# Rotary tables from eight transposes, their rows copied to the partitions by DMA, and one ordering dependence on VectorE

## The chip, the cores and the metric

The kernel runs on one core of one Trainium2 chip. The metric is the device time of one execution in microseconds (us). The engines of a core are TensorE (PE: matmuls and transposes; PEld: its weight loads), VectorE (DVE), ScalarE (ACT), GpSimd (POOL) and SyncE (SP, which here issues all DMAs). PSUM, where PE writes, has eight banks; several parts of the kernel compete for them.

## The reference

One decoder block on x of 1024 tokens by 1024 channels, float32:

```python
h = rms_norm(x, g_attn_pre) * (1 + sc_a) + sh_a      # sc_a, sh_a, ...: silu(c) @ w_ada + b_ada
proj = h @ w_in                                      # 1024 -> 2304
qa, ka = partial_rope(...), partial_rope(...)        # mixer A: 8 query heads, 2 key heads
qb, kb = partial_rope(...), partial_rope(...)        # mixer B: 8 heads
...                                                  # windowed attention A (sinks), dilated mixture B
x = x + gt_a * rms_norm(concat(norm(oa), norm(ob)) @ w_out, g_attn_post)
h = rms_norm(x, g_mlp_pre) * (1 + sc_m) + sh_m
x = x + gt_m * rms_norm(square(relu(h @ w_up)) @ w_down, g_mlp_post)
```

What the change touches is the rotation. It turns 16 of the 64 channels of each query and key head, by cos and sin of position times eight frequencies:

```python
rot = concat([x1 * cos - x2 * sin, x2 * cos + x1 * sin])   # x1, x2: 8 channels each
```

## The kernel before

**Precision.** Each float32 operand of a matmul is split into a high part (rounded on ScalarE) and a low part (the rest, by VectorE or GpSimd). A product is three matmuls: high by high, low by high, high by low (L875, L876, L878 in the projections).

**Layout.** Projections put channels on partitions and tokens on the free axis. The columns of w_in are ordered so that the channels to be rotated, of queries and keys alike, lie in the first of the three 128-channel chunks (c = 0) of each of six units u (two of mixer A, four of mixer B). Tokens go in two halves x = 0, 1 of 512. The rotation (f_rope, L768 to L775) is four VectorE instructions with two tables `tabs[0]` (cos) and `tabs[1]` (plus and minus sin), each 128 partitions by 1024 tokens, with the scale of the scores (-0.125 for queries, 1 for keys) multiplied in. Partitions that aren't rotated have cos 1 and sin 0, times that scale.

**The tables.** cos and sin are computed with tokens on partitions: `cosw` (128 x 8 blocks x 8 frequencies) and `sinw`, which holds minus sin at index 0 and sin at 1. `tables()` (L712 to L735) turns them. For each i (0: cos, 1: sin) GpSimd fills a tile "rows" of 128 x 8 x 128 by a memset and 8 to 10 copies of 64 elements (L719, L725), one for each place to which a frequency goes; PE transposes each of the eight blocks, four to a PSUM bank "ptab" (L731), and ScalarE copies a bank into the table with the scale of its partition (L733). This is done twice: before the first unit, for mixer A's order of channels (units 0 and 1), in the two PSUM banks of tag "t"; and before unit 2, for mixer B's order, in the bank of tag "x". The first transposes wait for `e_hh[3, 1]`, the high part of the fourth channel chunk. Each call makes four groups of four transposes and four ScalarE copies.

**The planner.** The order of each engine's instructions is fixed when the program is built, by a small planner (`Sched`). Each step has a duration, events it waits for (deps), buffers that it takes and gives back (`Res`, such as r_t for the two "t" banks), and a prio. For ACT, DVE, POOL and SP it picks the step with the earliest start, then the lowest prio, then the oldest. PE has named streams, each first in, first out; among streams whose head is ready, the order is post, misc, mod, fin, xt, tab, then dense ahead of or behind the attention. A step that can't have its buffer isn't ready. While PE would idle before the first matmul of the second token half, dummy matmuls on ones ("fillers", L892) are put in.

**The start, to about 70 us.** The x blocks come in, ScalarE squares them, GpSimd computes rstd (L467, L469), and PE transposes the scaled blocks into banks "t" (L640, stream xt), which ScalarE or VectorE copies to xnT (L644). The modulation is computed in four groups of two channel chunks: VectorE sums w_ada times silu(c) (L660, L662: four steps of two instructions), PE reduces over partitions (L670), VectorE finishes scale and shift (L676 to L678), then ScalarE writes the high part hw (L699, event e_hh) and the full value (L696), both with prio 0, and VectorE the low part (L702, event e_hl). The first group of chunks (k = 0, 1) is done for each token half by itself, the others for both. The first unit (first_unit) accumulates six results at once, x = 0, 1 by c = 0, 1, 2, in six PSUM banks; its order is x = 0 with k = 0, 1, then x = 1 with k = 0, 1, then k = 2 to 5 for all, then k = 6, 7 accumulator by accumulator. The sixth accumulator (x = 1, c = 2) is one of the two "t" banks:

```python
acc_at = [(pj, "pj", r_pj)] * 2 + [(po, "o", r_o)] + [(psp, "s", r_s)] * 2 + [(pt, "t", r_t)]
```

**After that** projections of the next units run beside the attention of earlier ones (to about 360 us), then the output projection, then the MLP as a fast matrix product with seven multiplications. SP issues all loads and stores in the planner's order: weights (w_st, L540), modulation weights (wa, L520; wa_st, L1008), parts of queries and keys sent to their places (kt, qt, L818).

Of the kernel before, what the change touches and what calls it, by code (L numbers as in the profile page):

```python
# [19 lines left out]
P = 128  # L20
# [304 lines left out]
def t_ps(n):  # L325
    return 0.055 + 0.00083 * n
# [10 lines left out]
def t_dv(n):  # L337
    return 0.066 + 0.00104 * n
# [19 lines left out]
def hybrid_block(ctx: ExitStack, tc: tile.TileContext, x, positions, w_ada, b_ada, g_attn_post, w_in, w_out,  # L358
# [128 lines left out]
    def r_in(a):  # L487
        return r_stg if a in beside else r_wa
# [125 lines left out]
    e = op("DVE", 4.2, f_turns, [e_pos, e_c], prio=1)  # L614

    def f_sin():
        A.activation(sinw[:, :, 1], ang[:], AF.Sin)
        A.activation(cosw[:], kq[:], AF.Sin)
    e_xn, e_rs = [[], []], []
    e_sin = op("ACT", 0.5, f_sin, [e, e_sinset], prio=1)  # L620
    e_rope = op("DVE", 0.15, lambda: V.tensor_scalar(sinw[:, :, 0], sinw[:, :, 1], -1.0, None, ALU.mult), [e_sin],
                prio=1)

    def x_block(tb):
# [21 lines left out]
                                    gives=[(r_t, 1)], prio=2))  # L646

    e_hh, e_hl = {}, {}
    def mod_group(g):

        b = {}
        e = e_cond
        c = slice(2 * g, 2 * g + 2)
        for j in range(4):
            def f(j=j):
                for n in range(2):
                    w, cj = wa_t[g, j][:, 512 * n:512 * n + 512], cond[:, 2 * j + n:2 * j + n + 1]
                    if j == n == 0:
                        b["acc"] = p0.tile([P, 512], F32, name="acc_a", tag="acc_a", bufs=2)
                        V.tensor_scalar(b["acc"][:], w, cj, None, ALU.mult)  # L660
                    else:
                        V.scalar_tensor_tensor(b["acc"][:], w, cj, b["acc"][:], ALU.mult, ALU.add)  # L662
# [24 lines left out]
    def mod_chunk(k, eg, half):  # L687
        t0, t1 = (0, TB) if half is None else (4 * half, 4 * half + 4)
        n = (t1 - t0) * P
        h = xnT[:, k, t0 * P:t1 * P].rearrange("p (x t) -> p x t", t=512)  # L690
        hh, hl = (hw[:, t0 // 4 * 4 + k // 2:t1 - 3 + k // 2:4, i, k % 2 * 512:k % 2 * 512 + 512] for i in range(2))
        deps = [eg] + (e_xn[0] + e_xn[1] if half is None else e_xn[half])

        def full(eng):
            if eng is A:
                return lambda: A.activation(h, h, AF.Identity, bias=s_a[:, k:k + 1], scale=g_a[:, k:k + 1])  # L696
            return lambda: V.tensor_scalar(h, h, g_a[:, k:k + 1], s_a[:, k:k + 1], ALU.mult, ALU.add)

        eh = op("ACT", t_sb(n) + 2 * AP_COST, lambda: A.activation(hh, h, AF.Identity, bias=s_a[:, k:k + 1],  # L699
                                                                  scale=g_a[:, k:k + 1]), deps, prio=0)  # L700
        e = op("ACT", t_sb(n) + 2 * AP_COST, full(A), [eh], prio=0)
        e = op("DVE", t_dv(n), lambda: V.tensor_tensor(hl, h, hh.bitcast(F32), ALU.subtract), [e],  # L702
               prio=0)
        for x in (0, 1) if half is None else (half,):
            e_hh[k, x], e_hl[k, x] = eh, e

# [2 lines left out]
    for g in range(4):  # L709
        mod_group(g)  # L710

    def tables(groups, place, r_place, r_bank, bank, deps):  # L712

        for i in range(2):
            b = {}

            def f_rows(i=i, b=b):
                t = b["t"] = place(i)
                G.memset(t, 0.0 if i else 1.0)  # L719
                for o, step, h in groups:  # L720
                    for x in range(2):
                        src = sinw[:, :, 1 - x] if i else cosw[:]
                        o_ = o + 64 * x
                        for j in range(h):
                            G.tensor_copy(t[:, :, o_ + j * step:o_ + j * step + (8 * h - h) * step + 1:h * step], src)  # L725
            e = op("POOL", 4.0, f_rows, [e_rope] + e_rs, takes=[(r_place, 1)] if r_place else [], prio=0)
            for x in range(2):
                def f_t(x=x, b=b):
                    b[x] = bank()
                    for j in range(4):  # L730
                        T.transpose(b[x][:, j], b["t"][:, 4 * x + j], ident)  # L731
                d = pe_op("tab", 0.43, f_t, [e, e_hh[3, 1]], takes=[(r_bank, 1)], gives=[(r_place, 1)] if x and r_place else [])
                e_tab[x].append(op("ACT", t_ps(512) + AP_COST, lambda i=i, x=x, b=b: A.mul(  # L733
                    tabs[i][:, 512 * x:512 * x + 512], b[x][:].rearrange("p b t -> p (b t)"), scl[0]), [d] + deps[x],
                                   gives=[(r_bank, 1)], prio=2))  # L735

    e_tab = [[], []]
    tables([(0, 2, 4), (1, 8, 1)], lambda i: vring.tile([P, TB, P], F32, name="rows", tag="v"), r_v, r_t,
           lambda: pt.tile([P, 4, P], F32, name="ptab", tag="t"), [[], []])


    op("ACT", 1.6, lambda: A.activation(warm[:], nhalf[:], AF.Exp), [e_sin] + [e_hl[KC - 1, x] for x in range(2)],
# [224 lines left out]

# [1211 lines left out]
```

## Time and profile before

| | |
|---|---|
| median of 3 runs (lowest to highest) | 1128.47 us (1128.34 to 1129.39) |
| the profiled execution: time | 1129.15 us |
| the profiled execution: span of its instructions | 1127.1 us |
| mean granted TensorE clock | 0.996 |
| table transposes (L731) | 32, 272 ns median |
| table copies on ScalarE (L733) | 8, 688 ns median |
| "rows" on GpSimd: memsets, copies | 4 and 36 |
| DMA | 193.69 MB, all issued by SP |

How to read it: a line of a timeline gives start, length, engine, line of the kernel, operation, output <- inputs, shape and count, and in brackets how long the engine idled before it and which instruction ended that. A matmul's length (390 ns for 512 columns) is longer than the distance to the next, because matmuls overlap; the distance from start to start is what one costs. A line of a tile view gives lowest, median and highest duration in ns. The table of stretches gives the busy time of PE, the granted clock, the share of DMA and GB/s.

### The profile page before, as it was taken

Reading aid. Unit: us, or ns where it says so; the run is one execution under the profiler, and the core shown is the slowest. Engines: PE = TensorE matmul, PEld = TensorE weight load, DVE = VectorE, ACT = ScalarE, POOL = GpSimd, SP = SyncE. Lnnn points to the kernel's source line nnn. Section 1 sums busy time; section 2 is a strip of 40 time slices with the busy share of each in tenths; the row PEclk is TensorE's granted clock in tenths of the full one; section 3 lists DMA queues with packets and bytes.
Section 4 is the critical chain, followed back from the end, with each engine's and each line's share of the span. In section 5 each row is a group of like instructions: output and inputs, shape, how many; then the busy total and the mean of one; then the engine's idle time right before and its main releaser. Section 6 shows DMA issues by size and latency. Waiting matters only on the chain.

```text
span 1127.1 us, 15613 instructions
## 1 busy us (share of the span) xinstructions
PE 1107.0 (98%) x5417; PEld 920.9 (82%) x5417; DVE 817.2 (73%) x1379; ACT 636.8 (56%) x1111; POOL 255.4 (23%) x336
## 2 busy tenths in 40 slices
PE   8999999999999999999999999999999999999997
PEld 6788888888888788788888888888888888888885
DVE  7968767666686576579889564798743996537998
ACT  8769767455665576677575334653145632246542
POOL 2447777567751131110000000000000000000003
PEclk9999999999999999999999999999999999999999
DMA  9564665554513642565861268711578112584104
GB/s 349 177 215 132 196 225 194 178 173 153 197 43 146 232 147 80 203 235 213 321 242 38 76 233 310 249 52 42 186 252 318 38 56 95 199 307 165 38 19 150
DMA packets 93215, 193.69 MB, mean 172 GB/s; under 512 B 8656, under 2 KB 31312, under 8 KB 93136
## 3 DMA queue, kind: packets, MB, share of 16 engines
q1 hardware_dynamic: 93136, 192.69, 49.2%
q8 instruction: 43, 0.70, 0.3%
q14 instruction: 36, 0.29, 0.1%
HBM read 141.28 MB, written 32.51 MB: 154 GB/s over the span
## 4 chain that ended last, share of the span: by engine, by line
PE 77%; ACT 7%; DVE 6%; DMA 3%; issue 3%; POOL 3%; SPq 1%; POOLq 0%; DVEq 0%; ACTq 0%
PE mlp_ps L1992 17%; PE mlp_ps L1991 17%; PE mlp_ps L1993 17%; PE pj L875 3%; PE pj L878 3%; PE pj L876 3%; PE s_ps L1139 3%; PE o_ps L1274 2%; PE y_ps L1545 2%; PE y_ps L1547 2%; PE y_ps L1546 1%; PE pt_ps L1244 1%; ACT p_sb L1214 1%; PE pt_ps L1247 1%; DMA o_sb<-o_dram 1%
## 5 line engine op out<-in xcount | busy, mean ns | idle before, releaser
L1991 PE MATMUL mlp_ps<-hw 128*128 128x512 f32 x896 | 349.6, 390 | 0.0
L1993 PE MATMUL mlp_ps<-hw 128*128 128x512 f32 x896 | 348.6, 389 | 0.0
L1992 PE MATMUL mlp_ps<-hw 128*128 128x512 f32 x896 | 348.6, 389 | 0.0
L1991 PEld LDWEIGHTS mlp_ps<-hw 128*128 128x128 f32 x896 | 168.2, 188 | 35.8 <-issue 0.5
L1992 PEld LDWEIGHTS mlp_ps<-hw 128*128 128x128 f32 x896 | 168.2, 188 | 35.2 <-issue 0.5
L1993 PEld LDWEIGHTS mlp_ps<-hw 128*128 128x128 f32 x896 | 168.2, 188 | 34.9
L1755 DVE TENSOR_TENSOR hw<-w,hw 128x1024 fp32r<-128x1024 f32 x96 | 114.6, 1219 | 95.2 <-ACT hw L1748 93.2
L1748 ACT CAST hw<-w 128x1024 fp32r<-128x1024 f32 x96 | 97.6, 1048 | 130.0 <-PE mlp_ps L1993 97.5
L2101 POOL TENSOR_TENSOR st<-st,nhalf 128x1 f32<-128x1 f32 x8 | 8.0, 1011 | 592.6 <-DVE st L2099 592.6
L875 PE MATMUL pj<-hw,w_hl 128*128 128x512 f32 x240 | 101.8, 424 | 0.0
L878 PE MATMUL pj<-hw,w_hl 128*128 128x512 f32 x240 | 94.7, 394 | 0.0
L876 PE MATMUL pj<-hw,w_hl 128*128 128x512 f32 x240 | 94.3, 393 | 0.0
L1262 DVE TENSOR_TENSOR ph<-pt_ps,ph 128x512 fp32r<-128x512 f32 (+1 forms) x110 | 68.2, 647 | 24.7 <-ACT ph L1258 24.5
L1748 ACT CAST hw<-u 128x1024 fp32r<-128x1024 f32 x48 | 48.7, 1052 | 64.6 <-PE mlp_ps L1993 64.6
L1258 ACT CAST ph<-pt_ps 128x512 fp32r<-128x512 f32 (+1 forms) x110 | 57.3, 557 | 24.1 <-PE pt_ps L1247 20.3
L1755 DVE TENSOR_TENSOR hw<-u,hw 128x1024 fp32r<-128x1024 f32 x48 | 57.0, 1218 | 18.2 <-ACT hw L1748 18.2
L1165 ACT ACTIVATE p_sb<-p_sb,mn 128x128 f32<-128x128 f32 (+3 forms) x64 | 49.7, 777 | 35.1 <-DVE mn L1158 32.2
L1170 POOL TENSOR_SCALAR p_sb<-p_sb,den 128x128 f32<-128x128 f32 (+3 forms) x64 | 49.0, 771 | 74.1 <-DVE den L1168 66.3
L2049 DVE TENSOR_TENSOR yacc<-yacc,mlp_ps 128x512 f32<-128x512 f32 x96 | 62.1, 681 | 3.3 <-PE mlp_ps L1993 3.3
L1024 POOL TENSOR_TENSOR ada_acc<-ada_acc,wa_st 128x512 f32<-128x512 f32 x42 | 55.8, 1328 | 3.5
L1545 PE MATMUL y_ps<-hw,oh 128*128 128x512 f32 x128 | 52.6, 411 | 0.9 <-DVE mn L1158 0.4
L878 PEld LDWEIGHTS pj<-hw,w_hl 128*128 128x128 f32 x240 | 45.1, 188 | 10.3
(207 smaller groups left out, 1994.1 us busy)
## 6 DMA issues: line engine op xcount, KB each, us to landing
hw<-s_dram SPq DMA_DIRECT2D x84, 512.0 KB, 4.3
wa_st<-in_w_ada SPq DMA_DIRECT2D x32, 512.0 KB, 4.3
w<-in_w_up SPq DMA_DIRECT2D x32, 512.0 KB, 5.5
w<-in_w_down SPq DMA_DIRECT2D x32, 512.0 KB, 6.8
s_dram<-hw SPq DMA_DIRECT2D x28, 512.0 KB, 3.2
qt<-hl SPq DMA_DIRECT2D x40, 256.0 KB, 2.6
w_st<-in_w_in SPq DMA_DIRECT2D x36, 256.0 KB, 3.1
x_sb<-in_x SPq DMA_DIRECT2D x16, 512.0 KB, 5.6
```

The lines of the kernel that those rows point to most:

```text
L875: T.matmul(ps, w[:, 0, n], h[0], start=(k == 0), stop=False)
L876: T.matmul(ps, w[:, 1, n], h[0], start=False, stop=False)
L878: T.matmul(ps, w[:, 0, n], h[1], start=False, stop=(k == KC - 1))
L1258: A.copy(b["ph"][:, 0, :w], b["pt"][:, :w])
L1262: V.tensor_tensor(b["ph"][:, 1, :w], b["pt"][:, :w], b["ph"][:, 0, :w].bitcast(F32), ALU.subtract)
L1545: T.matmul(ps[:], b["oh"][:, k], wh[:, c0:c0 + 512], start=(k == 4 * m), stop=False)
L1748: A.copy(out[j][0], flat(src[j]))
L1755: V.tensor_tensor(out[j][1], flat(src[j]), out[j][0].bitcast(F32), ALU.subtract)
L1991: T.matmul(ps[m][:], sh, mh, start=starts and k == 0, stop=False, **kw)
L1992: T.matmul(ps[m][:], sh, ml_, start=False, stop=False, **kw)
L1993: T.matmul(ps[m][:], sl, mh, start=False, stop=k == 3, **kw)
L2049: e = op("DVE", t_dv(512), lambda: V.tensor_tensor(y(), y(), ps[m][:], ALU.add), [e, ml.e_y[tb, n]], gives=gives, prio=1)
```

## The change

`sinw` now has sin at index 0 and minus sin at 1. GpSimd writes one tile "turned" of 128 tokens x 8 blocks x 64 columns: cos twice and sin, minus sin, each once with the factor -0.125 and once without. Eight transposes, of 64 columns each, turn it, in two groups of four; ScalarE copies the two results (64 partitions x 512) to a tile "rows" in SBUF. They wait for the turned tile and for `e_hh[1, 0]`, and take the "t" banks. GpSimd fills the tables with their values for partitions that aren't rotated. For mixer A ten DMAs copy the 16-row groups of "rows" to every eighth partition of the tables. For mixer B four DMAs, when unit 1's second chunk is queued, write the rows to DRAM in that mixer's order (`rot_dram`); before unit 2 GpSimd fills each half of the tables again, after unit 1's rotation of that half, and four DMAs a half bring the rows in, with no transposes.

The second part: the low part (L702) of the third pair of chunks (k = 4, 5) is made to follow the last step of the modulation sums (group 3, step 3) on VectorE, by an event `last_acc` that is set when the planner places that step.

```diff
     def f_sin():
-        A.activation(sinw[:, :, 1], ang[:], AF.Sin)
+        A.activation(sinw[:, :, 0], ang[:], AF.Sin)
...
-                   takes=[(r_acc, 1)] if j == 0 else [], gives=[(r_in((g, j)), 1)], prio=1)
+                   takes=[(r_acc, 1)] if j == 0 else [], gives=[(r_in((g, j)), 1)], prio=1,
+                   after=partial(setattr, last_acc, "t", 0.0) if (g, j) == (3, 3) else None)
...
-        e = op("DVE", t_dv(n), lambda: V.tensor_tensor(hl, h, hh.bitcast(F32), ALU.subtract), [e],
-               prio=0)
+        e = op("DVE", t_dv(n), lambda: V.tensor_tensor(hl, h, hh.bitcast(F32), ALU.subtract),
+               [e] + ([last_acc] if k // 2 == 2 else []), prio=0)
...
-    def tables(groups, place, r_place, r_bank, bank, deps):
...
+    def f_turned():
+        t = b_tab["t"] = early.tile([P, 1024], F32, name="turned", tag="early")[:, 0:512].rearrange(
+            "p (b g r) -> p b g r", b=TB, g=4)
+        for y in range(2):
+            G.tensor_copy(t[:, :, 1, 8 * y:8 * y + 8], cosw[:])
+        G.tensor_copy(t[:, :, 3].rearrange("p b (y f) -> p b y f", y=2), sinw[:])
+        for i in (0, 2):
+            G.tensor_scalar(t[:, :, i], t[:, :, i + 1], -0.125, 1.0, ALU.mult, ALU.mult)
+    e_turned = op("POOL", 1.8, f_turned, [e_rope] + e_rs, prio=0)
+
+    def init_tabs(cs):
+        n = cs.stop - cs.start
+        G.tensor_copy(tabs[0][:, cs], scl[0].to_broadcast([P, n]))
+        G.memset(tabs[1][:, cs], 0.0)
...
+    def tables_a():
+        e_tab0 = op("POOL", 1.9, lambda: init_tabs(slice(0, 1024)), [e_c, e_turned], prio=0)
...
+            def f_t(x=x):
+                b_tab[x] = pt.tile([P, 4, P], F32, name="ptab", tag="t")
+                for j in range(4):
+                    T.transpose(b_tab[x][:64, j], b_tab["t"][:, 4 * x + j].rearrange("p g r -> p (g r)"), ident)
+            d = pe_op("tab", 0.43, f_t, [e_turned, e_hh[1, 0]], takes=[(r_t, 1)])
+
+            def f_r(x=x):
+                if not x:
+                    b_tab["r"] = early.tile([P, 1024], F32, name="rows", tag="early")
+                A.copy(b_tab["r"][:64, 512 * x:512 * x + 512], b_tab[x][:64].rearrange("p b t -> p (b t)"))
+            e_rows.append(op("ACT", t_ps(512), f_r, [d], gives=[(r_t, 1)], prio=2))
+
+        def f_rows_a():
+            for i in range(2):
+                for o in (0, 2, 4, 6, 1):
+                    r = 32 * i + 16 * (o % 2)
+                    nc.sync.dma_start(tabs[i][o:o + 121:8], b_tab["r"][r:r + 16])
+        e = load(f_rows_a, 655360, e_rows + [e_tab0], prio=-13, n=10)
...
+    def store_rows():
...
+                    nc.sync.dma_start(dst[p], b_tab["r"][r:r + 16].unsqueeze(1).to_broadcast([16, 2, 1024]))
+        e_rotd[:] = [load(f_rows_d, 524288, list(e_rotd), prio=16, n=4)]
+
+    def tables_b():
+        for x in range(2):
+            cs = slice(512 * x, 512 * x + 512)
+            e = op("POOL", 1.1, lambda cs=cs: init_tabs(cs), [e_rot[1, x]], prio=0)
+
+            def f_rows(cs=cs):
+                for i in range(2):
+                    for y in range(2):
+                        nc.sync.dma_start(tabs[i][64 * y:64 * y + 32, cs], rot_dram[i, 32 * y:32 * y + 32, cs])
+            e_tab[x].append(load(f_rows, 262144, [e] + e_rotd, prio=-13, n=4))
...
+            if (u, x, c) == (1, 0, 1):
+                store_rows()
             if (u, x, c) == (2, 0, 0):
...
-                tables([(0, 1, 4)], lambda i: stage("rows")[:].rearrange("p (b r) -> p b r", b=TB), r_stg, r_x,
-                       lambda: px.tile([P, 4, P], F32, name="ptab", tag="x"), [[e_rot[1, 0]], [e_rot[1, 1]]])
+                tables_b()
```

More of the change, by code (lines that the diff above doesn't have):

```diff
@@ L620, in hybrid_block @@
     e_sin = op("ACT", 0.5, f_sin, [e, e_sinset], prio=1)
-    e_rope = op("DVE", 0.15, lambda: V.tensor_scalar(sinw[:, :, 0], sinw[:, :, 1], -1.0, None, ALU.mult), [e_sin],
+    e_rope = op("DVE", 0.15, lambda: V.tensor_scalar(sinw[:, :, 1], sinw[:, :, 0], -1.0, None, ALU.mult), [e_sin],
                 prio=1)
@@ L648, in hybrid_block @@
     e_hh, e_hl = {}, {}
+    last_acc = Ev()
     def mod_group(g):
@@ L710, in hybrid_block @@
         mod_group(g)
-    def tables(groups, place, r_place, r_bank, bank, deps):
[L714 to L735, printed above, removed]
@@ L737, in hybrid_block @@
-    e_tab = [[], []]
-    tables([(0, 2, 4), (1, 8, 1)], lambda i: vring.tile([P, TB, P], F32, name="rows", tag="v"), r_v, r_t,
-           lambda: pt.tile([P, 4, P], F32, name="ptab", tag="t"), [[], []])
+    b_tab = {}
+    rot_dram = dram.tile([2, 64, 1024], F32, name="rot_dram")
+    def f_turned():
[6 more added lines that the diff above has]
+            G.tensor_scalar(t[:, :, i], t[:, :, i + 1], -0.125, 1.0, ALU.mult, ALU.mult)
@@ new lines, in hybrid_block @@
+    e_turned = op("POOL", 1.8, f_turned, [e_rope] + e_rs, prio=0)
[3 more added lines that the diff above has]
+        G.memset(tabs[1][:, cs], 0.0)
+    e_tab, e_rotd = [[], []], []
+    def tables_a():
+        e_tab0 = op("POOL", 1.9, lambda: init_tabs(slice(0, 1024)), [e_c, e_turned], prio=0)
+        e_rows = []
+        for x in range(2):
[15 more added lines that the diff above has]
+        e = load(f_rows_a, 655360, e_rows + [e_tab0], prio=-13, n=10)
+        for x in range(2):
+            e_tab[x].append(e)
+        e_rotd.extend(e_rows)
@@ new lines, in hybrid_block, with f_rows_d @@
+    tables_a()
+    def store_rows():
+        def f_rows_d():
+            for i in range(2):
+                dst = rot_dram[i].rearrange("(r j p) n -> p r j n", j=2, p=2)
+                for p in range(2):
+                    r = 32 * i + 16 * p
+                    nc.sync.dma_start(dst[p], b_tab["r"][r:r + 16].unsqueeze(1).to_broadcast([16, 2, 1024]))
+        e_rotd[:] = [load(f_rows_d, 524288, list(e_rotd), prio=16, n=4)]
+    def tables_b():
+        for x in range(2):
+            cs = slice(512 * x, 512 * x + 512)
+            e = op("POOL", 1.1, lambda cs=cs: init_tabs(cs), [e_rot[1, x]], prio=0)
+            def f_rows(cs=cs):
+                for i in range(2):
+                    for y in range(2):
+                        nc.sync.dma_start(tabs[i][64 * y:64 * y + 32, cs], rot_dram[i, 32 * y:32 * y + 32, cs])
+            e_tab[x].append(load(f_rows, 262144, [e] + e_rotd, prio=-13, n=4))
```

## The prediction

> **What bounds the kernel now.** I read the head and the slices of the page first, then the stretches of TensorE, then the tile view of the table transposes, then the timelines of TensorE and ScalarE around them.
>
> ```profile
> span 1127.1 us, 15613 instructions
> PE 1107.0 (98%) x5417; PEld 920.9 (82%) x5417; DVE 817.2 (73%) x1379; ACT 636.8 (56%) x1111; POOL 255.4 (23%) x336
> ```
>
> ```profile
> 70.00:120.00 50.00, 48.82 (x276) 1.00 0.60 185
> 120.00:160.00 40.00, 39.83 (x224) 1.00 0.59 186
> 160.00:460.00 300.00, 297.07 (x1684) 0.99 0.48 163
> ```
>
> TensorE (PE) is the bound: 98% of the span, and in the stretches (columns: stretch, its length, PE busy, matmuls, granted clock, DMA share, GB/s) it idles 1.2, 0.2 and 2.9 us. So an edit is worth what it takes from or puts into PE's stream once that is dense; the other engines matter only where PE waits for them. That stream becomes dense at 37.85 us, after the last real wait:
>
> ```profile
> 34.74 0.39 PE L875 MATMUL acc<-hw,w_hl 128*128 128x512 f32 x1
> ...
> 35.20 0.40 PE L875 MATMUL acc<-hw,w_hl 128*128 128x512 f32 x1
> 35.43 0.39 PE L876 MATMUL acc<-hw,w_hl 128*128 128x512 f32 x1
> 35.66 0.39 PE L875 MATMUL acc<-hw,w_hl 128*128 128x512 f32 x1
> ...
> 37.85 0.98 PE L878 MATMUL acc<-hw,w_hl 128*128 128x512 f32 x3 [1.56 <-DVE hw L702]
> ...
> 39.13 0.60 PE L731 MATMUL ptab<-head,rows 128*128 128x128 f32 x4
> 39.49 0.48 PE L875 MATMUL acc<-hw,w_hl 128*128 128x512 f32 x1
> 39.80 0.39 PE L876 MATMUL acc<-hw,w_hl 128*128 128x512 f32 x1
> 40.03 0.40 PE L875 MATMUL acc<-hw,w_hl 128*128 128x512 f32 x1
> ...
> 41.65 0.64 PE L731 MATMUL ptab<-head,rows 128*128 128x128 f32 x4
> ```
>
> The three pairs at 34.74, 35.20 and 35.66 open the accumulators of the second token half (x=1), c = 0, 1, 2; one pair takes 0.46 us (35.20 less 34.74).
>
> **What the transposes cost PE.** From 39.13 to 40.03 lie one group of four transposes and one pair: 0.90 less 0.46 is 0.44 us a group.
>
> ```profile
> L731 PE MATMUL ptab<-head,rows x32: 270/272/329, 39.1 to 143.1; 128*128 128x128 f32 x32
> ```
>
> 32 transposes are eight groups; by the code four belong to the first call of tables(), all after 37.85, and four to the second, the last at 143.1, in a stretch where PE is busy 39.83 of 40 us. The second four go for good: 4 x 0.44 = 1.76 us less. The first four leave the dense stretch too, another 1.76 us less. The two new groups (the same four matmuls each, with 64 columns instead of 128 of weights, so between nothing and 0.44 us a group) come earlier, and where they come decides the case; in the dense stretch they would cost up to 0.88 us.
>
> **Where the two new groups fall.** The old groups waited for e_hh[3, 1], which ScalarE writes in the 36.38 row below; the new ones wait for e_hh[1, 0], long done, and for the turned rows that GpSimd writes where it now writes the old rows, after the last rstd.
>
> ```profile
> 30.13 0.95 POOL L719 MEMSET rows<- 128x1024 f32 x1
> 31.14 3.10 POOL L725 COPY rows<-cosw 128x64 f32<-128x64 f32 x10
> ...
> 35.16 4.28 POOL L725 COPY rows<-sinw 128x64 f32<-128x64 f32 x10
> ```
>
> Five instructions replace 22. At 0.31 us a 64-wide copy (3.10 / 10) and up to twice that for the three that are 128 wide, they take 1.6 to 2.5 us, so the rows are ready at about 32 to 32.6. Then the groups need a bank of the two "t" banks (r_t), which the last x transposes hold until ScalarE has read them:
>
> ```profile
> 32.58 1.08 ACT L644 COPY xnT<-pxt 128x512 f32<-128x512 f32 x2 [0.22 <-PE pxt L640]
> 33.54 1.53 ACT L699 ACTIVATE hw<-xnT,s_a,g_a 128x512 fp32r<-128x512 f32 x2
> 34.96 1.51 ACT L696 ACTIVATE xnT<-xnT,s_a,g_a 128x512 f32<-128x512 f32 x2
> 36.38 2.36 ACT L699 ACTIVATE hw<-xnT,s_a,g_a 128x1024 fp32r<-128x1024 f32 x2
> 38.64 2.36 ACT L696 ACTIVATE xnT<-xnT,s_a,g_a 128x1024 f32<-128x1024 f32 x2
> 40.91 0.67 ACT L733 ACTIVATE tab<-ptab,head 128x512 f32<-128x512 f32 x1
> ```
>
> These two copies free the banks at about 33.1 and 33.7. PE has nothing else then, "tab" stands ahead of "dense" in its order, so both groups run before 34.74 and hold both banks. There PE ran fillers, so the two groups cost it nothing. But the accumulator of x=1, c=2 (the pair at 35.66) is itself a "t" bank. It must now wait until ScalarE has copied a group out. ScalarE's queue is fixed by the planner: earliest start, then the lower prio. The two modulation pairs (L699, L696) have prio 0 and stand ready one behind the other from 33.54 to 41.00; the new row copies have prio 2. The first group ends after the first L699 has its start, since the bank it needs is freed at 33.1 and four transposes with their hand-overs take longer than the one xnT copy left (0.5 us). So the first row copy lands where the first L733 landed, at 40.91. Its price is that of ScalarE's 64x512 copy out of PSUM:
>
> ```profile
> 67.74 0.59 ACT L840 COPY vt<-acc 64x512 f32<-64x512 f32 x1
> ```
>
> It ends at 41.50. After the first L733 (ends 41.58) the next group started at 41.65, 0.07 later; that this bank, read by ScalarE, releases PE is in the rows above. So the pair of x=1, c=2 starts at 41.57 instead of 35.66, and the L878 behind it at 42.03 instead of 37.85: 4.18 us later. All "dense" matmuls are one first-in first-out stream, and nothing else of PE is ready. Against it stand the four old groups, 1.76 us: after the first unit PE is 2.42 us late. With the 1.76 us of the second set: +0.66 us.
>
> **What the idle does to PE.** PE now stands from 35.82 (end of the second pair) to 41.57, 5.8 us, and no fillers run, since they end with the first x=1 matmul. What such a gap does, the trace bounds: the gap of 1.56 us at 37.85 left the pitch at 0.23 us (half a pair's 0.46), so nothing is the lower end; the upper end is the start, where PE came from standing.
>
> ```profile
> 1.50 2.08 PE L892 MATMUL acc<-ones_r 128*128 128x512 f32 x4 [1.50 <-DVE nhalf L579]
> ```
>
> ```profile
> 1.50 8.39 PE L892 MATMUL acc<-ones_r 128*128 128x512 f32 x26 [1.50 <-DVE nhalf L579]
> ```
>
> ```profile
> L892 PE MATMUL acc<-ones_r x61: 387/395/796, 1.5 to 34.4; 128*128 128x512 f32 x61
> ```
>
> The first four fillers have a pitch of (2.08 - 0.80) / 3 = 0.43 us; the 26 take 8.39 - 0.39 = 8.00 us where 25 pitches of 0.23 would take 5.75: 2.25 us lost. A gap of 5.8 us is nearly four times the one that did no harm, so I take 2.25. A gain is excluded, since no row runs faster than 0.23. The Trainium skill, "TensorE: Matmul & The Clock Gate", Part 1, has the clock halved after an idle window of some 3.4 us and restored after a busy one as long; by it the loss is an estimated 1.7 us or more, +2.4 us in all, and since the windows run free, an idle of 5.8 us holds a whole one about 7 times in 10. The start of this trace agrees (0.43 against 0.23 us); no row shows a gap of that length later.
>
> **The sum.** +0.66 + 2.25 = +2.91 us. The profiled execution took 1129.15 us, 2.05 more than its span; with the change 1132.1. The median of the runs is 0.68 lower, so I forecast 1131.4.
>
> **What lies beside.** ScalarE loses eight L733 (8 x 0.67 = 5.4 us) and gains two copies; DVE's work is the same, with the sign moved to the other half. GpSimd loses the 9.3 us from 30.13 on and 18 instructions of the second set, and gains short fills of the tables; nothing of PE waits for either. The last modulation sum stands ahead of the third pair's low parts already:
>
> ```profile
> 47.82 3.11 DVE L662 SCALAR_TENSOR_TENSOR acc_a<-wa,cond,acc_a 128x512 f32<-128x512 f32 x4
> 50.84 2.35 DVE L702 TENSOR_TENSOR hw<-xnT,hw 128x1024 fp32r<-128x1024 f32 x2
> ...
> 58.01 2.36 DVE L702 TENSOR_TENSOR hw<-xnT,hw 128x1024 fp32r<-128x1024 f32 x2 [2.98 <-ACT xnT L696]
> ```
>
> Without the last L733 (0.67 us) ScalarE would deliver the third pair up to 0.7 us sooner, and its low part (1.2 us) could slip in ahead of the sum; the new dependence forbids that. It keeps the order of before, so it costs nothing, and waits behind it only in DVE's queue, as before.
>
> SP gets ten table copies, of 64 KB, between the last modulation loads and the next weights.
>
> ```profile
> 35.78 3.97 SPq L520 DMA_DIRECT2D wa<-in_w_ada  x8
> 45.53 0.34 SPq L540 DMA_DIRECT2D w_st<-in_w_in  x1
> 69.33 3.81 SPq L818 DMA_DIRECT2D qt<-hl  x6
> ```
>
> ```profile
> o_dram<-ot SPq DMA_DIRECT2D x64, 64.0 KB, 2.1
> ```
>
> ```profile
> 54.36 0.67 DVE L554 TENSOR_TENSOR w_hl<-w_st,w_hl 128x512 fp32r<-128x512 f32 x1
> 62.34 0.68 DVE L772 TENSOR_TENSOR hl<-acc,tab 64x512 f32<-64x512 f32 x1 [1.96 <-PE acc L878]
> ...
> 142.47 0.68 DVE L772 TENSOR_TENSOR hl<-pj,tab 64x512 f32<-64x512 f32 x1 [2.85 <-ACT tab L733]
> ```
>
> The second row copy ends at 42.1, after the modulation loads have gone (39.75). At 0.6 us an issue (3.81 / 6) the ten take 42.2 to 48.3, and land by 50.4 (2.1 from issue to landing for 64 KB), 12 us ahead of the first rotation (62.34). The w_st load of 45.53 is 2.8 us later; its split comes 9 us behind it on DVE (54.36), so this costs nothing; if that cover were gone, up to 2.8. The store (four issues) and the second tables (eight, 4.8 us on SP) take the place of chains that now keep DVE 2.85 us waiting for L733 at 142.47 without PE standing still.
>
> The order of all later work is planned anew. PE's idle in the three stretches is 4.3 us; I let a third of it, 1.3 us, go either way.
>
> **The rivals.** First, the stall without the lost clock: +0.66, so 1129.1. For it: only the start shows a slow pitch, and what length of idle brings it back no row tells. Second, the other side: the row copies come ahead of the modulations on ScalarE, or the pair at 35.66 has its bank first. Then no bank is missing, both sets are gain, and the table groups lie among fillers. The first set's 1.76 us is cut by the next bound, the low part of k=7, ready at 58.01 + 2.36 = 60.37:
>
> ```profile
> 61.91 0.39 PE L878 MATMUL acc<-hw,w_hl 128*128 128x512 f32 x1
> ```
>
> That leaves 1.5 us less a hand-over of 0.1: 1.4. With 1.76: -3.2, so 1125.3. It decides if a row copy starts before 36.7: with 0.59, 0.07 and 0.46 the pair then ends ahead of the 37.85 at which L702 lets PE go on anyway. For it: the place in ScalarE's queue hangs on two hand-overs between engines that no row shows alone. Against it: prio 0 is ready without a break for 7.4 us. Third, forecast and a late second table: the four copies of a half must follow GpSimd's fill and cross a busy SP queue; if the rotation is late by more than a tile, PE stands; an estimate of 2 us from the 2.85 of waiting above: 1133.4.
>
> **How the numbers follow.** Forecast 0.53, stall with the clock held 0.21, no stall 0.21, late table 0.05. That the number of transposes falls to eight can't fail. 0.2% is 2.3 us, about what a measurement of this kernel can tell from no change. With 1.3 us either way the forecast passes +2.3 in about 7 of 10 (0.37), the late table does (0.05), the held clock hardly (0.02): slower 0.44. No stall passes -2.3 in 8 of 10, 0.17, and 0.01 from the held clock: faster 0.18. Same 0.38. The range reaches from the middle of the no-stall case, 1125.2, to 1133.4, leaving about 0.15 out; the likeliest case alone is 1130.1 to 1132.7.
>
> **What would show it.** Eight transposes of 64 columns in two groups near 33 to 35; behind two pairs of x=1 a PE idle of 5 to 6 us, released by a ScalarE copy of 64x512 near 41; then a dozen matmuls at a pitch of 0.43; the L878 of 61.91 reached some 4.7 us later; no table transposes up to 143. If PE goes on at 37.85, or the row copies stand before 36.7 on ScalarE, the forecast is wrong and the second rival right; if the idle is there and the pitch after it stays 0.23, the first.

## The result, and the profile after

The changed kernel takes 1122.36 us (median of 6 runs, 1121.29 to 1122.91), against 1128.4 us for the kernel before beside it: ratio 0.995, 95% interval 0.9939 to 0.9961. That is 6 us less, where 2.9 us more was forecast. The profiled execution took 1121.29 us. The head of its page:

```profile
span 1119.4 us, 15555 instructions
PE 1103.2 (99%) x5393; PEld 917.0 (82%) x5393; DVE 820.4 (73%) x1381; ACT 629.6 (56%) x1095; POOL 246.7 (22%) x315
```

PE has 24 instructions fewer (32 transposes gone, 8 new) and is busy 3.8 us less, but the span is 7.7 us shorter: more went than the work taken out. The first stretches of the kernel after (length, PE busy, matmuls, granted clock, DMA share, GB/s):

```profile
70.00:120.00 50.00, 49.61 (x285) 1.00 0.65 198
120.00:160.00 40.00, 40.00 (x222) 1.00 0.66 209
```

PE's idle time in them is 0.39 and 0 us (before: 1.18 and 0.17). Now the place for which the stall was forecast, in the PE timeline of the kernel after:

```profile
32.17 1.04 PE L741 MATMUL ptab<-head,turned 128*64 128x128 f32 x8
...
33.51 0.94 PE L673 MATMUL pm<-ones,acc_a 128*128 128x1 f32 x8
...
34.63 0.39 PE L917 MATMUL acc<-hw,w_hl 128*128 128x512 f32 x1
...
35.85 0.50 PE L917 MATMUL acc<-hw,w_hl 128*128 128x512 f32 x1
...
36.98 0.97 PE L920 MATMUL acc<-hw,w_hl 128*128 128x512 f32 x3 [0.39 <-DVE hw L705]
```

Both new groups run at 32.17, among the fillers (now L934), ahead of the second modulation reduction (L673). The pair of the sixth accumulator, forecast for 41.57, starts at 35.85; PE then waits 0.39 us for the low part and goes on at 36.98. ScalarE's timeline shows why:

```profile
33.82 1.51 ACT L699 ACTIVATE xnT<-xnT,s_a,g_a 128x512 f32<-128x512 f32 x2
35.23 1.05 ACT L747 COPY rows<-ptab 64x512 f32<-64x512 f32 x2
36.17 0.63 ACT L549 CAST w_hl<-w_st 128x512 fp32r<-128x512 f32 x1
37.73 0.62 ACT L549 CAST w_hl<-w_st 128x512 fp32r<-128x512 f32 x1 [0.93 <-DMA w_st<-in_w_in]
38.25 2.37 ACT L702 ACTIVATE hw<-xnT,s_a,g_a 128x1024 fp32r<-128x1024 f32 x2
```

The row copies (L747) stand right behind the first modulation pair. The second pair (L702), at 36.38 before without a gap, starts at 38.25 only. It needs VectorE's finish of scale and shift (L679 to L681), which in the kernel after ends at 37.86; the last 0.4 us it stands behind a weight cast (L549). VectorE in the kernel after:

```profile
34.79 1.53 DVE L664 SCALAR_TENSOR_TENSOR acc_a<-wa,cond,acc_a 128x512 f32<-128x512 f32 x2
36.24 1.29 DVE L705 TENSOR_TENSOR hw<-xnT,hw 128x512 fp32r<-128x512 f32 x2
37.44 0.15 DVE L679 TENSOR_TENSOR g_a<-pm,bb 128x2 f32<-128x2 f32 x1
...
37.71 0.15 DVE L681 TENSOR_TENSOR s_a<-pm,bb 128x2 f32<-128x2 f32 x1
```

and in the kernel before, where it stood ahead of the sum and the low parts:

```profile
35.25 0.15 DVE L676 TENSOR_TENSOR g_a<-pm,bb 128x2 f32<-128x2 f32 x1
...
35.60 1.56 DVE L662 SCALAR_TENSOR_TENSOR acc_a<-wa,cond,acc_a 128x512 f32<-128x512 f32 x2
37.08 1.36 DVE L702 TENSOR_TENSOR hw<-xnT,hw 128x512 fp32r<-128x512 f32 x2
```

So ScalarE had a hole of two and a half microseconds, and the planner put the row copies into it, with two weight casts behind them. The reduction itself is no later in the trace (33.51 us, against 33.52 for L670 before): what moved is the order, which the planner fixes from its own estimates of time, and those stand in no trace. In exchange the low parts (L705) come 0.84 us earlier than before (36.24 against 37.08), and PE goes on 0.87 us earlier (36.98 against 37.85). That gain had no place in the forecast.

**Where the time went.** The start of the same matmul in several kernels, in us against its start in the profile of before (matmuls counted in the traces; 48th, 96th ... are low-by-high matmuls of the projections, L876 before):

| kernel | 48th | 96th | 120th | 192nd | 288th, the last | first of the MLP | last of the MLP |
|---|---|---|---|---|---|---|---|
| before, start | 68.48 | 130.88 | 160.86 | 253.09 | 381.01 | 504.86 | 1117.88 |
| after | -1.83 | -3.20 | -5.33 | -5.95 | -5.83 | -7.83 | -7.80 |
| late copies | +6.03 | +4.57 | +2.07 | +1.03 | +1.01 | -1.16 | -1.17 |
| groups after the reduction | +5.71 | +3.96 | +2.16 | +1.13 | +1.34 | -0.98 | -0.96 |
| no transposes, same order | -1.06 | -0.21 | -1.93 | -1.94 | -0.98 | -3.01 | -3.02 |
| eight matmuls back | -1.15 | -2.60 | -2.94 | -3.59 | -3.42 | -5.90 | -5.92 |

The start scatters: in executions with the same order up to the 48th matmul, the first pair of x = 1 stands at 34.0 to 34.7 us (three with before's order) and at 34.6 to 35.4 (five with that of after). So half a microsecond between two rows says nothing by itself. Two things can be read from the table. The change has its whole gain, 5.8 us, by the 192nd matmul. And the 2 us between the last projection and the MLP aren't the change's: every kernel run here, those with before's own order among them, shows 1.9 to 2.8 us there. They lie in before's one profiled execution, in windows of one us (PE's busy time is the second figure, the granted clock the one behind the bracket):

```profile
383.00:384.00 1.00, 0.56 (x3) 1.00 1.01 404
384.00:385.00 1.00, 0.47 (x2) 1.00 0.36 139
385.00:386.00 1.00, 1.00 (x6) 0.54 0.15 51
...
387.00:388.00 1.00, 1.00 (x4) 0.50 0.41 53
388.00:389.00 1.00, 1.00 (x5) 0.75 0.90 315
```

The windows put the half clock from 385.1 to 388.5 us; these 3.4 us cost 1.7. That is why the two profiles differ by 7.7 us and the medians by 6.0. A part of the 6.0 is probably lost clock too: of the 60 executions of before beside the later runs, those with a mean clock of 0.996 or less took 1127.7 to 1131.9 us and the others 1126.4 to 1128.2, and four of the six here lie above 1128.3. The second run of the change, below, has 5.4.

### The profile page after: what moved, and what is told of

It is laid out like the page before. It is cut to its first block, busy times and chain, and to the rows that moved or that the text cites. A ratio compares the mean times of both kernels' runs of the same rounds, so it can differ in the third digit from the quotient of the medians.

```text
span 1119.4 us, 15555 instructions
## 1 busy us (share of the span) xinstructions
PE 1103.2 (99%) x5393; PEld 917.0 (82%) x5393; DVE 820.4 (73%) x1381; ACT 629.6 (56%) x1095; POOL 246.7 (22%) x315
## 4 chain that ended last, share of the span: by engine, by line
PE 83%; DVE 8%; issue 3%; DMA 2%; ACT 1%; SPq 1%; POOL 1%; POOLq 0%; DVEq 0%; ACTq 0%
PE mlp_ps L2034 17%; PE mlp_ps L2035 17%; PE mlp_ps L2036 17%; PE pj L917 4%; PE pj L920 4%; PE pj L918 4%; PE s_ps L1182 3%; PE y_ps L1588 2%; PE y_ps L1590 2%; PE y_ps L1589 2%; PE o_ps L1317 2%; PE s_ps L1237 1%; PE pt_ps L1287 1%; PE o_ps L1329 1%; PE pt_ps L1294 1%
```

## The experiments

My theory after the result: the two groups, ahead of the reduction on PE, push the second modulation back in the planner's order; that opens the hole on ScalarE, and the stall never arises; the removed PE work is worth about its 3.5 us (2 x 1.76); and what the time shows beyond it is chance in the order planned anew. The rivals: the stall never threatened; or the new event or the new dependence brings the gain. Ratios are against the kernel before on the same chip, with 95% intervals.

**The change once more.**

> The changed kernel once more, as the common yardstick. Theory A (the gain is PE time: 1.8 us in the first unit, 1.76 us in the second set, the rest fewer waits in a newly planned attention part): 5.5 to 6.5 us under the kernel before. Rival B (a part of the measured 6 us is a throttled stretch that the kernel before happened to have at 380 to 400 us): under 5 us.

Measured: 1122.02 us, ratio 0.9949 (0.9937 to 0.9962). The gain is there again, 5.4 us, a little under theory A's 5.5 to 6.5 and above rival B's 5, and its trace agrees (-5.65 at the 120th matmul, -8.07 at the end, in the terms of the table).

**Late copies.** The row copies wait for the second modulation pair, where the forecast had them:

```diff
-            e_rows.append(op("ACT", t_ps(512), f_r, [d], gives=[(r_t, 1)], prio=2))
+            e_rows.append(op("ACT", t_ps(512), f_r, [d, e_hh[3, 1]], gives=[(r_t, 1)], prio=2))
```

> The two row copies on ScalarE are made to wait for the high part of the fourth chunk, which puts them where the prediction saw them, behind both modulation pairs. The mechanism of the prediction: PE idles 5 to 6 us behind two pairs of the second half, released by a row copy near 41; against the changed kernel that costs 4.2 us (5.0 if measured from its own start of that matmul), and 2.25 more if PE's pitch is 0.43 for a while after. Rival: the planner finds other work for PE, or the low parts of the first chunks come as late anyway, and it costs under 2 us.

Measured: 1130.22 us, ratio 1.0021 (1.0012 to 1.0030), 8.2 us above the change run again (6.5 to 7.3 had been expected with the lost clock). PE and ScalarE in this run:

```profile
42.68 1.84 PE L673 MATMUL pm<-ones,acc_a 128*128 128x1 f32 x8 [6.37 <-DVE acc_a L664]
...
44.38 0.77 PE L917 MATMUL acc<-hw,w_hl 128*128 128x512 f32 x1
...
47.09 0.63 PE L918 MATMUL acc<-hw,w_hl 128*128 128x512 f32 x1
47.52 0.63 PE L917 MATMUL acc<-hw,w_hl 128*128 128x512 f32 x1
```

```profile
39.01 2.37 ACT L702 ACTIVATE hw<-xnT,s_a,g_a 128x1024 fp32r<-128x1024 f32 x2
...
43.55 1.04 ACT L747 COPY rows<-ptab 64x512 f32<-64x512 f32 x2
```

and PE's windows:

```profile
46.00:48.00 2.00, 2.00 (x7) 0.50 0.66 102
48.00:50.00 2.00, 2.00 (x10) 0.91 0.64 102
```

With the copies behind both modulation pairs, PE does stand (6.37 us), and it does come back at half clock, with a pitch of 0.43 us (47.52 less 47.09), until about 48.4. What ends the idle is not yet a copy but the next reduction, released by VectorE's sums; the projections go on at 44.38, behind the first copy. The second pair is late here too (39.01 us, forecast 36.38), so PE stands longer than forecast. The mechanism of the forecast is real; it needs an order that the planner did not choose. That the median lies 2.8 us above before's, where the forecast had 2.9, is luck in part: in the profiled execution, the fastest of the ten, the first unit is 6.0 us late instead of 4.7, and by the last projection 5.0 have come back instead of 1.8.

**Groups after the reduction.** The groups wait for the second reduction instead of a long past event, so that they can't stand ahead of it:

```diff
-        ep = pe_op("mod", 0.9, pm, ...)
+        ep = e_pm[g] = pe_op("mod", 0.9, pm, ...)
...
-            d = pe_op("tab", 0.43, f_t, [e_turned, e_hh[1, 0]], takes=[(r_t, 1)])
+            d = pe_op("tab", 0.43, f_t, [e_turned, e_pm[1]], takes=[(r_t, 1)])
```

> The changed kernel, but the two transpose groups wait for the second modulation reduction on PE. Theory D (the forecast stall failed to come because the groups stand ahead of that reduction: it then is 0.65 us late in the plan, VectorE's finishing slips behind a 1.5 us sum, the second modulation pair isn't ready on ScalarE and the row copies get their place at 35): then the row copies go behind both modulation pairs again, PE idles 5 us, and the end of the first unit lies 6 to 8 us behind the changed kernel's. Rival (the copies' place has another reason): the first unit ends as in the changed kernel, within 1 us.

Measured: 1126.97 us, ratio 0.9999 (0.999 to 1.0009), 5 us above the change. PE, then ScalarE, then VectorE in this run:

```profile
33.28 1.05 PE L673 MATMUL pm<-ones,acc_a 128*128 128x1 f32 x8 [0.60 <-DVE acc_a L664]
...
34.98 1.04 PE L741 MATMUL ptab<-head,turned 128*64 128x128 f32 x8
...
40.53 0.79 PE L917 MATMUL acc<-hw,w_hl 128*128 128x512 f32 x1 [4.05 <-ACT rows L747]
```

```profile
35.38 2.37 ACT L702 ACTIVATE hw<-xnT,s_a,g_a 128x1024 fp32r<-128x1024 f32 x2
37.66 2.35 ACT L699 ACTIVATE xnT<-xnT,s_a,g_a 128x1024 f32<-128x1024 f32 x2
39.92 1.04 ACT L747 COPY rows<-ptab 64x512 f32<-64x512 f32 x2
```

```profile
34.93 0.15 DVE L679 TENSOR_TENSOR g_a<-pm,bb 128x2 f32<-128x2 f32 x1
```

This is the forecast's picture, with nothing asked of ScalarE's queue: the finish at 34.93, the second pair without a gap at 35.38, the row copies behind it at 39.92 (forecast 40.91), and PE released by them after 4.05 us. The first unit ends 7.5 us behind the kernel after, within the 6 to 8 expected, and 5.7 behind before (forecast 4.7), though the median ends level with before's: 4.4 of it come back by the last projection (+5.71 to +1.34). One step of PE's order, the groups ahead of the reduction or behind it, decides between stall and none.

**The old event.** The groups wait for the event of the old transposes:

```diff
-            d = pe_op("tab", 0.43, f_t, [e_turned, e_hh[1, 0]], takes=[(r_t, 1)])
+            d = pe_op("tab", 0.43, f_t, [e_turned, e_hh[3, 1]], takes=[(r_t, 1)])
```

> The changed kernel with the transposes waiting for the high part of the fourth chunk, as the old ones did. By theory A the two groups then lie in the dense stretch, 0.88 us, but PE at the end of the first unit stands at the low part of k = 7 anyway, so that end moves by under 0.9 us. The total is open to the order's scatter.

Measured: 1122.15 us, ratio 0.9954 (0.9941 to 0.9968). In PE's timeline the groups now lie in the dense stretch, and PE goes on nearly where it did before:

```profile
37.69 0.97 PE L920 MATMUL acc<-hw,w_hl 128*128 128x512 f32 x3 [1.39 <-DVE hw L705]
...
38.95 0.60 PE L741 MATMUL ptab<-head,turned 128*64 128x128 f32 x4
```

The medians of this run and of the change are 0.1 us apart, so the new event and the earlier groups aren't what makes the change faster: any place will do that keeps clear of the stall. The first unit does pay for the groups. Its 48th matmul starts at 67.42 us, 0.77 later than in the kernel after (66.65; the two groups cost 0.88 by the forecast), and no low part of k = 7 holds PE up near its end.

**No transposes, same order.** In the kernel before, the transposes are not issued, and ScalarE's table copies read the untransposed rows tile instead of the bank (so the tables are wrong); every other step keeps its place:

```diff
                 def f_t(x=x, b=b):
-                    b[x] = bank()
-                    for j in range(4):
-                        T.transpose(b[x][:, j], b["t"][:, 4 * x + j], ident)
+                    pass
...
-                    tabs[i][:, 512 * x:512 * x + 512], b[x][:].rearrange("p b t -> p (b t)"), scl[0]), [d] + deps[x],
+                    tabs[i][:, 512 * x:512 * x + 512], b["t"][:, 4 * x:4 * x + 4].rearrange("p b t -> p (b t)"), scl[0]), [d] + deps[x],
```

> The kernel before with its planned order, but the 32 table transposes left out; ScalarE reads the rows where it read the bank, so the tables are wrong. The price of the transposes by itself: 1.76 us for the second set and 1.4 to 1.8 for the first (cut by the low part of k=7): 3.2 to 3.5 us under before if PE time counts one to one. Rival: PE time doesn't count one to one because other engines bound the attention part: under 2 us.

Measured: 1126.2 us, ratio 0.9985 (0.9976 to 0.9994), so 0.7 to 2.7 us. By the table the second set is worth 1.72 us where it stood (-0.21 to -1.93): 1.76 had been worked out. But the first set's 1.06 is half an earlier start (the first pair of x = 1 stands at 34.25 us, 34.74 before) and is given back by the 96th matmul, and another 0.95 goes by the last projection. Among the waits of PE from 30 to 500 us one has grown from 0.3 us (L846 before) to 1.8 (us in all, times, longest):

```profile
PE pv L844 <- ACT vt L838: 1.8, 2, 1.0
```

In an order planned with the transposes, PE without them runs into other engines, and 3.5 us of PE work bring 1.2 in the medians: under 2 us, as the rival had it.

**Eight matmuls back.** The reverse: the kernel after, with eight more 128x512 matmuls at the first accumulations of unit 2, whose results are overwritten at once; the order stays:

```diff
+                    i, n = w_at(u, c, 0)
+                    for _ in range((3, 3, 2)[c] if (u, x) == (2, 0) else 0):
+                        T.matmul(b[0][:], w_hl[u, i][:, 0, n * P:n * P + P], hw[:, 4 * x, 0, 0:512], start=True, stop=True)
```

> The changed kernel in its own order with eight more 128x512 matmuls (8 x 0.23 = 1.84 us of PE, the price of 16 transposes) at the three projections of unit 2's first half; their results are overwritten. Theory A (PE time counts one to one there): 1.84 us above the changed kernel, so about 1123.9. Rival (PE has slack from the order's waits): under 0.8 us above.

Measured: 1123.03 us, ratio 0.9962 (0.995 to 0.9975). Between the 96th and the 120th matmul it loses 1.8 us against the change run again (0.92 to 2.71 us behind it), which is eight times 0.23: the stretch is dense. In the medians it is 1.0 us, between the two forecasts, and the intervals of both runs overlap.

**The first set only.** The kernel after, with mixer B's tables by the old `tables()`:

```diff
-            if (u, x, c) == (1, 0, 1):
-                store_rows()
...
-                tables_b()
+                tables([(0, 1, 4)], ...)
```

> Mixer A's tables as in the changed kernel, mixer B's as before (16 transposes, GpSimd rows, ScalarE copies). Theory A: the first unit gains 1.8 us as in the changed kernel, the second set nothing: 1.8 us under before, up to 2 us either way from the new plan. Rival C (nearly all of the gain sits in what the second set blocked: GpSimd rows of 6 us, ScalarE copies, a PSUM bank): also about 1.8 under before, but the changed kernel then lies 4 us or more below this one, with the waits of PE at 120 to 160 us back.

Measured: 1134.49 us, ratio 1.0058 (1.0045 to 1.0072): 12.5 us above the change for 1.8 us of transposes. The longest of PE's waits from 30 to 500 us, and the stretch in which it lies:

```profile
PE o_ps L1341 <- ACT ph L1325: 3.3, 1, 3.3
```

```profile
180.00:200.00 20.00, 16.65 (x76) 0.88 0.61 197
```

In a stretch that begins 35 us after the last transpose (145.4), PE waits 3.3 us for ScalarE's high part of the attention weights (L1325), and loses clock there as well (0.88). ScalarE in the same stretch:

```profile
190.39 1.15 ACT L1434 ACTIVATE wo_hi<-wo_st,head 128x1024 fp32r<-128x1024 f32 x1 [4.09 <-POOL ada_acc L1091]
```

Ahead of that high part in its queue stands an output weight, which waited 4.1 us for GpSimd. The small edit made another order of everything behind it, and a bad one. So the total says nothing of the first set, and rival C (what the second set blocks) isn't decided by it either. The 48th matmul, ahead of the second set, starts at 66.93 us, within the range of the change (66.4 to 67.3 in five executions): the gain in the first unit is there with the first set alone.

**Four orders more.** How large is such chance? LEAD is a constant of the planner, 0.8, that says how far the projections may run ahead of the attention before PE prefers the attention. It changes no work, only the order; by the traces PE's order first differs at about 106 (0.82) and 110 us (0.78) in the kernel before, and at about 98 us in the kernel after. Here it is 0.82 and 0.78, in the kernel before and in the kernel after:

```diff
-    LEAD = 0.8
+    LEAD = 0.82
```

> The kernel before with the planner's limit for how far the projections may run ahead of the attention (LEAD) at 0.82 instead of 0.80: the same instructions, another order in the attention part. It measures what a new order alone is worth. Theory A (order is worth a few us either way, so 2 us of the gain beyond PE's own time may be order): 1 to 8 us from before, either sign. Rival (order is worth nothing, within 1 us of before): then all of the 6 us must come from work that was removed.

> As the run before, with 0.78: 1 to 8 us from before by theory A, within 1 us by the rival.

> The changed kernel with the limit at 0.82. Theory A: 3.5 us of the gain is PE time and stays; order moves it by some us either way, so 1117 to 1128. Rival: the 6 us stay within 1: 1121 to 1123.

> The changed kernel with the limit at 0.78: as the run before. If both changed variants lie below both variants of before by 2 to 4 us, the removed work is shown beyond the order's scatter.

| LEAD | before | after | ratio of the changed order to before's median |
|---|---|---|---|
| 0.8 | 1127.4 | 1122.0 | 0.9949 (0.9937 to 0.9962), after |
| 0.82 | 1132.1 | 1126.3 | 1.0044 (1.0029 to 1.0059), before; 0.9991 (0.9982 to 1.0001), after |
| 0.78 | 1127.3 | 1128.0 | 0.9998 (0.9988 to 1.0007), before; 1.0004 (0.9995 to 1.0013), after |
| mean | 1128.9 | 1125.4 | |

One kernel's times lie 4.9 us apart by order alone, and the other's 6.0; three of the four new orders moved the time by 4.3 to 6.0 us, and before with 0.78 stayed where it was, as the rival had it. Pair by pair the change brings 5.4 and 5.8 us and costs 0.7; in the mean it brings 3.5. The sign that had been named beforehand, both changed variants below both variants of before, did not come: 1128.0 lies above 1127.3. Three orders are few, so the 3.5 has an uncertainty of some two us; that it agrees with 2 x 1.76 fits work that counts one to one in the mean, and doesn't show it. With 0.82 before's loss is for the most part in PE's waits (70 to 500 us; the first was 0.6 us with 0.8, the second is not among its waits):

```profile
PE o_ps L1274 <- DVE ph L1262: 2.9, 5, 1.1
PE o_ps L1286 <- DVE v_hl L857: 1.3, 1, 1.3
```

**Without the new dependence.** The low parts of the third pair no longer wait for the last modulation sum:

```diff
-               [e] + ([last_acc] if k // 2 == 2 else []), prio=0)
+               [e], prio=0)
```

> The changed kernel without the dependence on the last modulation sum: the third pair's low parts go ahead of it on VectorE. The prediction had the guard at no cost and said that without it the last sum shifts by up to 2.4 us (two low parts of 1.2): the last modulated chunks come that much later, PE waits 1 to 2 us at k = 6, 7 of the first unit. Rival: PE isn't there yet and nothing changes before 60 us. The total is open to the order's scatter of some us.

Measured: 1122.93 us, ratio 0.9961 (0.9948 to 0.9975). VectorE in this run:

```profile
48.68 2.35 DVE L705 TENSOR_TENSOR hw<-xnT,hw 128x1024 fp32r<-128x1024 f32 x2
50.95 1.53 DVE L664 SCALAR_TENSOR_TENSOR acc_a<-wa,cond,acc_a 128x512 f32<-128x512 f32 x2
...
58.03 2.36 DVE L705 TENSOR_TENSOR hw<-xnT,hw 128x1024 fp32r<-128x1024 f32 x2 [3.58 <-ACT xnT L699]
```

against the last of these in the kernel after:

```profile
57.53 2.36 DVE L705 TENSOR_TENSOR hw<-xnT,hw 128x1024 fp32r<-128x1024 f32 x2 [2.98 <-ACT xnT L699]
```

Without it the low parts do slip in ahead of the sum, as had been said. The sum ends at 52.48 us, 2.1 later than in the kernel after (50.40), but there two low parts stood behind it, ahead of the finish (L681), which is only 0.5 us later (54.30 against 53.80); so is the last low part. PE waits 0.8 us for low parts of k = 7 (0.2 in the kernel after), where 1 to 2 had been expected. The dependence is worth about 0.5 us in the first unit; the two medians, 0.9 us apart, don't tell it from nothing.

## Why the prediction was wrong

**The step that failed.** "The two modulation pairs (L699, L696) have prio 0 and stand ready one behind the other from 33.54 to 41.00; the new row copies have prio 2", so "the first row copy lands where the first L733 landed, at 40.91". I took ScalarE's rows of before as fixed and asked only where the copies fit in. But I had put both groups ahead of 34.74 on PE, and the planner set them ahead of L673, the reduction on which the second pair depends. VectorE's finish then lost its place to a sum and two low parts (35.25 to 37.44), the second pair came at 38.25, and the copies had ScalarE at 35.23. The run with the groups after the reduction shows this cause by taking it away. It also shows that the rest of the chain (bank, sixth accumulator, one stream first in, first out) was right, since there a row copy releases PE; the run with late copies agrees. The condition that I gave the second rival, a row copy before 36.7, was met; what I named for it, "two hand-overs between engines", was not the reason.

**The lost clock: right in kind, too small in size.** 2.25 us was the term. In the run with late copies PE is back at work at 42.68 and at half clock to about 48.4, half of 5.7, or 2.9 us; with the groups after the reduction it is back at 40.53 and slow to about 50.0, which is 4.8 us. The Trainium skill, "TensorE: Matmul & The Clock Gate", Part 1, has the clock restored after about 3.4 us of sustained work. These two rows show 5.7 and 9.5 us, with no idle in either but a reduction of eight one-column matmuls (L673) in both, at 42.68 and at 45.39, so the page's figure is a lower end here.

**The first set** (1.76 us), cut to 1.4 us by the low part of k = 7: right as the next bound, and about right in size. PE in the kernel after still waits for that low part, a little, near the end of the first unit, though it now ends at 59.89 us instead of 60.37. The table's 1.83 us at the 48th matmul is one pair of executions: three with before's order have it at 67.7 to 68.5 us and five with that of after at 66.4 to 67.3, and the means lie 1.2 us apart.

```profile
59.94 0.50 PE L920 MATMUL acc<-hw,w_hl 128*128 128x512 f32 x1 [0.17 <-DVE hw L705]
```

**The second set** (1.76 us): right for the stretch where it stood, 1.72 in the run without transposes. What of it lasts to the end depends on the order.

**The places where nothing was to be lost: right.** The ten copies and the eight of the second tables in SP's rows of the kernel after, and the rotations behind them in VectorE's:

```profile
39.41 8.55 SPq L754 DMA_DIRECT2D tab<-rows  x10
...
123.96 4.68 SPq L780 DMA_DIRECT2D tab<-rot_dram  x8
```

```profile
60.53 0.68 DVE L814 TENSOR_TENSOR hl<-acc,tab 64x512 f32<-64x512 f32 x1 [0.65 <-PE acc L920]
...
138.16 0.68 DVE L814 TENSOR_TENSOR hl<-pj,tab 64x512 f32<-64x512 f32 x1
```

The copies took 8.55 us to issue instead of 6.1, began earlier than forecast, are out by 47.96 and landed some 4 us later, 8 us ahead of the first rotation at 60.53, which waits for PE and not for a table. Unit 2's rotation waits for nothing, where it waited 2.85 us for L733; so the third rival is out.

**The other term that was too small:** "I let a third of it, 1.3 us, go either way". The order of all later work moves the time by several us (the runs with LEAD). The no-stall case's 1125.3 us is near the mean of the three changed orders, 1125.4, though three orders are few; the measured 1122.4 is one of these, and a lucky one. By the two traces the 5.4 us to the start of the output projection (383.47 before, 378.09 after) are 3.6 us less PE work behind the first pair of x = 1 (343.9 to 340.3 us busy; eight groups of 0.44 are 3.5), 0.8 less idle from there to 70 us (1.56 to 0.75), 0.8 less idle behind that (3.3 to 2.5) and 0.1 from an earlier start. Ahead of that pair the new groups fill idle time. Which of the planner's choices spared the later idle wasn't tried.

## What to carry to other kernels

Before taking another engine's timeline as fixed, go through everything that the moved step now stands ahead of on its own engine, and follow each of those to the engine in question: the hole that it opens there may be the place for which you were looking. In a kernel whose order is planned statically, perturb the order without changing the work (here LEAD) before believing a gain or loss of a few us; work removed from the bounding engine need not count one to one in any one order (3.5 us brought 1.2 here with the order kept, and -0.7 to 5.8 with new orders). And compare profiles stretch by stretch: a difference that one execution shows against all other kernels belongs to that execution and not to the change.

## What the runs showed of the hardware

- The clock fell without a longer idle: in before's profile from 385.1 us on, after four us in which PE was busy 0.75, 0.99, 0.56 and 0.47 us and never idle for over 0.53 us at a time. That a PE that is merely thinly used can lose the clock had no place in my prediction.
- After a true idle the fall came at different delays, 1.8 us behind the last matmul in the run with late copies (idle from 36.31, half clock from about 38.1) and 3.4 us with the groups after the reduction (idle from 36.49, half clock from about 39.85). The half clock lasted 10.2 us in both; it was 3.4 us in before's profile and 6.8 in the run with the first set only (195.2 to 202.0), so once, twice and three times 3.4. How much of it PE feels depends on when it falls and when work returns: the run with the shorter idle (4.05 us against 6.37) had the longer slow stretch behind it.
- The ten small table copies took nearly twice as long to land as assumed: 3.9 us in the median against 2.1 for the 64 KB stores of before, from which I had it.

```profile
tab<-rows SPq DMA_DIRECT2D x10, 64.0 KB, 3.9
```
